# Gathering the experts' tokens in quarter rows with block transposes, and loading weights in 1 MB transfers

## The chip, the cores and the metric

The kernel runs on one core of a Trainium2 chip: TensorE (PE), VectorE (DVE), ScalarE (ACT), GpSimd (POOL), SyncE (SP) and 16 DMA engines. The metric is the device time of one execution in microseconds.

## The reference

One layer of a streaming encoder over 2048 tokens of width 1024: RMSNorm, one input projection, two groups of mixing heads (mLSTM and stick-breaking attention), an output projection, a mixture of experts, a gated per-layer term and a last RMSNorm. The part that matters here is the mixture of experts: every token goes to 2 of 32 experts, each expert is a SwiGLU of width 512.

```python
def expert_block(args):
    xb, e = args                                  # 128 rows of one expert
    hid = jax.nn.silu(xb @ w_gate[e]) * (xb @ w_up[e])
    return hid @ w_down[e]
y = lax.map(expert_block, (xin, block_e)).reshape(R, D)
out = jax.ops.segment_sum(y * buf_w[:, None], buf_tok, num_segments=T)
```

An expert has 6 MB of weights in float32: `w_gate` and `w_up` of 1024x512, `w_down` of 512x1024.

## The kernel before

All matmuls run in fp32r. A float32 operand is split into a high part (`hi`, a rounding copy on ScalarE, line 79) and a low part (`lo`, source minus `hi` on VectorE, line 80); a product is three matmuls, high by high, high by low, low by high (lines 88 to 90).

Phase 1 projects and runs the attention, phase 2 the mLSTM, the output projection and the router, phase 3 the experts, phase 4 the gated term and the output. Phase 2 writes the normed tokens to `c` in memory with four columns more: the two weights and the two experts of a token (line 834). At its end `route` builds tables of token indices: `toki` (whom to gather) and `tokd` (where to add), one column for each block of rows.

Phase 3 works on 47 blocks in a fixed order. The experts, ranked by their load, have fixed pieces: 128 rows, or 64 for the tail; 35 blocks have 128 rows and 12 have 64. Experts with several pieces and experts with one alternate. For each block:

- `xprep` (1079): GpSimd gathers the block's rows of `c` with one indirect DMA, one row of 4112 bytes to a partition, and forms the rows' weights `pw` with three tiny operations.
- `xturn` (1090): TensorE turns x in eight 128x128 transposes (1097) into two PSUM tiles, each of which is split into `xh` and `xl`.
- `gate_up` (1111): for each of 8 blocks of the width, 3 matmuls of 512 columns each for gate and up. In a block of 64 rows high and low lie side by side, 2 matmuls do, and the two halves of the result are added afterwards through `fold` tiles (1105).
- `hturn` (1139): the hidden rows are transposed by TensorE, four at a time, and split.
- `down` (1152): the product with `w_down`; the result goes to `y` and is added to `h` in memory by an indirect DMA of GpSimd (1174).

The loop over blocks (1205) interleaves them: in block b's `gate_up` the previous block's `hturn` stands before k = 3 and the next block's `xturn` before k = 6; after it comes the previous block's `down`. The scheduler of the framework may move instructions of an engine within the bounds of their inputs and buffers.

Weights come from `load_expert` (1071) on SyncE's queue: twelve pieces of 512 KB, each two blocks of 128 rows of gate or up (rows of 2 KB) or one of down (rows of 4 KB). `piece` (1250) lands one in one of five raw buffers (`wraw`: two in pool a, three in pool b), and splits it into `wh` and `wl`, 8 buffers each per pool. SyncE issues a load when VectorE has made `wl` of the piece that held the buffer.

After the experts `load4` (1262) loads the gate weights of phase 4 by the same `piece`, and a loop for overflowing experts follows that does not run on these inputs.

## Time and profile before

| | us |
|---|---|
| median of 3 runs | 2561.73 |
| lowest, highest | 2558.21, 2576.3 |
| profiled execution | 2559.68 |
| its span, first to last instruction | 2557.8 |

| engine | busy us of the span | share |
|---|---|---|
| TensorE matmuls | 2403.7 | 94% |
| VectorE | 1731.0 | 68% |
| ScalarE | 1294.0 | 51% |
| GpSimd | 657.5 | 26% |

The profile is of one execution, taken by the hardware profiler. A busy share is an average over stages with different limits; what an engine waited for is inferred from semaphores. Matmuls are pipelined, so a matmul's own duration is longer than the distance to the next. The expert stage runs from about 1540 to 2345 us of the span. A group's line gives the count, the busy time, the mean of one in ns, the engine's idle time just before them and what ended most of it. DMA packets are the rows that a transfer is cut into; a queue's share is the time that its packets took, over 16 engines.

### The profile page before, as it was taken

How to read it: one execution, taken by the hardware profiler on the slowest of the kernel's cores; microseconds unless marked ns; L12 is line 12 of the kernel's file. 1: busy time of each engine (PE TensorE's matmuls, PEld its weight loads, DVE VectorE, ACT ScalarE, POOL GpSimd, SP SyncE). 2: the span in 40 equal slices, each digit the busy share in tenths (PEclk: the TensorE clock that was granted, in tenths of full speed). 3: DMA queues.
4: the chain of work that ended last, by engine and by line, in shares of the span. 5: the costliest groups of instructions: out<-in, count | busy, mean ns of one | idle time of the engine just before them, and what ended most of it. 6: DMA issues, size and time to landing. Idle time of an engine off the chain costs nothing.

```text
span 2557.8 us, 36511 instructions
## 1 busy us (share of the span) xinstructions
PE 2403.7 (94%) x12620; PEld 1987.6 (78%) x12620; DVE 1731.0 (68%) x2628; ACT 1294.0 (51%) x2243; POOL 657.5 (26%) x777
## 2 busy tenths in 40 slices
PE   7899999999998899978999989999999999998998
PEld 6787787787876888967888767788877788786887
DVE  4488988988777445215555477777777787786665
ACT  5355656555555222223322366666666666675443
POOL 1122322322211230011111123232232333331654
PEclk9999999999999899989999999999999999998999
DMA  5776675675553532166666349999999999998332
GB/s 168 188 192 169 165 188 155 180 188 146 145 146 87 165 116 51 73 169 181 171 166 179 119 178 308 293 299 323 285 311 313 301 327 313 302 307 272 123 125 99
DMA packets 326038, 510.64 MB, mean 200 GB/s; under 512 B 40348, under 2 KB 163356, under 8 KB 324316
## 3 DMA queue, kind: packets, MB, share of 16 engines
q1 hardware_dynamic: 216044, 353.23, 42.2%
q0 software_dynamic: 97616, 123.05, 20.6%
q10 hardware_dynamic: 12192, 32.02, 3.5%
q8 instruction: 100, 1.64, 0.3%
q14 instruction: 86, 0.70, 0.1%
HBM read 389.63 MB, written 118.59 MB: 199 GB/s over the span
## 4 chain that ended last, share of the span: by engine, by line
PE 43%; DMA 11%; ACT 3%; issue 3%; DVE 3%; POOL 1%; SPq 0%; ACTq 0%; DVEq 0%; POOLq 0%
PE ppx L90 7%; PE ppx L88 7%; PE ppx L89 7%; DMA wraw<-in_w_exp_gate_dram 3%; DMA wraw<-in_w_exp_down_dram 3%; PE ps L88 2%; PE ps L90 2%; PE ps L89 2%; DMA md<-gr 2%; PE pw L89 2%; PE pw L90 2%; PE pw L88 2%; DMA wraw<-in_w_exp_up_dram 2%; ACT wh L79 2%; DVE wl L80 1%
## 5 line engine op out<-in xcount | busy, mean ns | idle before, releaser
L80 DVE TENSOR_TENSOR wl<-wraw,wh 128x1024 fp32r<-128x1024 f32 x384 | 458.9, 1219 | 132.6 <-ACT wh L79 129.1
L79 ACT CAST wh<-wraw 128x1024 fp32r<-128x1024 f32 x384 | 396.2, 1051 | 213.8 <-DMA wraw<-in_w_exp_gate_dram 78.7
L88 PE MATMUL ppx<-wh,xh 128*128 128x512 f32 x816 | 329.7, 405 | 5.8 <-ACT wh L79 5.0
L90 PE MATMUL ppx<-wh,xl 128*128 128x512 f32 x816 | 323.2, 396 | 2.8 <-DVE xl L80 2.7
L89 PE MATMUL ppx<-wl,xh 128*128 128x512 f32 x816 | 321.9, 395 | 0.5 <-DVE wl L80 0.5
L88 PE MATMUL ps<-aTh,whi 128*128 128x512 f32 x640 | 257.5, 403 | 6.6 <-ACT whi L79 3.3
L79 ACT CAST ph<-pt 128x512 fp32r<-128x512 f32 (+1 forms) x320 | 167.5, 523 | 180.1 <-PE pt L398 175.6
L90 PE MATMUL ps<-aTh,wlo 128*128 128x512 f32 x640 | 255.0, 398 | 0.7 <-DVE wlo L80 0.7
L89 PE MATMUL ps<-aTl,whi 128*128 128x512 f32 x640 | 255.5, 399 | 0.0
L385 DVE TENSOR_TENSOR_SCAN prod<-keep,prod,zeros 128x512 f32<-128x512 f32 x192 | 245.0, 1276 | 11.3 <-PE pt L398 5.8
L80 DVE TENSOR_TENSOR pl<-pt,ph 128x512 fp32r<-128x512 f32 (+1 forms) x320 | 190.1, 594 | 46.5 <-ACT ph L79 46.1
L380 ACT ACTIVATE keep<-pz 128x512 f32<-128x512 f32 (+2 forms) x320 | 171.5, 536 | 56.0 <-PE pz L378 46.7
L90 PEld LDWEIGHTS ppx<-wh,xl 128*128 128x128 f32 x816 | 154.1, 189 | 41.0 <-DVE xl L80 6.3
L88 PEld LDWEIGHTS ppx<-wh,xh 128*128 128x128 f32 x816 | 154.4, 189 | 40.0 <-ACT wh L79 5.3
L398 PE MATMUL pt<-ident,prod 128*128 128x128 f32 x1088 | 173.0, 274 | 11.6 <-DVE pl L80 10.1
L398 PEld LDWEIGHTS pt<-ident,prod 128*128 128x128 f32 x1088 | 134.0, 139 | 61.6 <-DVE pl L80 23.6
L89 PEld LDWEIGHTS ppx<-wl,xh 128*128 128x128 f32 x816 | 154.5, 189 | 33.3 <-DVE wl L80 1.0
L370 POOL DMA_DIRECT2D dv<-dv x80 | 60.9, 761 | 413.1 <-PE ot L411 338.6
L1174 POOL DMA_INDIRECT h<-y,tokd x47 | 119.8, 2550 | 164.1 <-DVE y L1173 63.4
L88 PE MATMUL ps<-whi,aTh 128*128 128x260 f32 (+1 forms) x512 | 145.0, 285 | 13.8 <-ACT whi L79 13.8
L88 PEld LDWEIGHTS ps<-aTh,whi 128*128 128x128 f32 x640 | 121.5, 190 | 32.6 <-ACT whi L79 4.3
L90 PEld LDWEIGHTS ps<-aTh,wlo 128*128 128x128 f32 x640 | 121.6, 190 | 31.2 <-DVE wlo L80 3.5
(320 smaller groups left out, 5439.6 us busy)
## 6 DMA issues: line engine op xcount, KB each, us to landing
wraw<-in_w_exp_gate_dram SPq DMA_DIRECT2D x128, 512.0 KB, 6.0
wraw<-in_w_exp_up_dram SPq DMA_DIRECT2D x128, 512.0 KB, 5.9
wraw<-in_w_exp_down_dram SPq DMA_DIRECT2D x128, 512.0 KB, 6.9
kt<-k POOLq DMA_DIRECT2D x80, 512.0 KB, 5.1
dv<-dv POOLq DMA_DIRECT2D x80, 256.0 KB, 3.4
k<-pst SPq DMA_DIRECT2D x64, 256.0 KB, 4.2
wraw<-in_w_in_dram SPq DMA_DIRECT2D x32, 256.0 KB, 4.1
q<-pst SPq DMA_DIRECT2D x32, 256.0 KB, 3.7
```

The source lines that it names most:

```text
L79: first = nc.scalar.copy(hi, src)
L80: nc.vector.tensor_sub(lo, src, f32(hi))
L88: mm(ps, lh, rh, start=start, stop=False)
L89: mm(ps, lh, rl, start=False, stop=False)
L90: return mm(ps, ll, rh, start=False, stop=stop)
L370: nc.gpsimd.dma_start(dv, self.dv2[m][4 * s:4 * s + 4, :, e, :].rearrange("i p d -> p i d"))
L380: nc.scalar.activation(kk[:, :w], ps[:, :w], AF.Sigmoid, scale=-0.125)
L385: nc.vector.tensor_tensor_scan(pr[:, :w][:, ::-1], kk[:, :w][:, ::-1], zeros[:, :w], 1.0 if s == t else carry[j][:, 0:1], ALU.mult, ALU.add)
L398: nc.tensor.transpose(pt[:, i * P:(i + 1) * P], pr[i][:, j * P:(j + 1) * P], self.ident)
L1174: nc.gpsimd.indirect_dma_start(out=self.hd_[:, :], out_offset=bass.IndirectOffsetOnAxis(ap=idx[:n], axis=0), in_=y[:n], in_offset=None, co ...
```

## The change

Five edits belong together.

1. Phase 2 writes the tokens to `c` with 1024 columns and the four extra columns to a tensor of their own, `inf`. `route` makes a table `qui` beside `toki`: for partition 32q + t and group g the index of quarter row q of token 32g + t of a block. Some tables move from a pool that lives on to one that ends with phase 2.
2. `xload` gathers a block's x by `qui`: for each 32 tokens one indirect DMA of 128 quarter rows of 1 KB, four in a block of 128 rows and two in one of 64, and one more for the 16 bytes of `inf`.
3. `xturn` is one VectorE transpose of 32x32 blocks into `xt` instead of eight on TensorE; ScalarE copies `xt` to `xh`, GpSimd subtracts to get `xl`. Partition p then holds columns 8p to 8p + 7 of x. `xt` and the `fold` tiles share one buffer. `turned` of block b + 1 stands before k = 2, and `load` of block b + 2 behind it.
4. So that rows of the weights match, gate and up are read with 8 neighbouring rows on a partition, down with 4; hidden columns are read with a stride of 4 from PSUM (`by4`). `pair` loads two pieces in one transfer of 1 MB, 8 KB in a row to a partition, into three raw buffers of 1 MB (one in pool a, two in b) instead of five of 512 KB, and splits each half as before.
5. `load4` loads the gate weights of phase 4 by `pair`.

```diff
-        self.cd_ = self.mk("c", [S, D + 4])
+        self.cd_ = self.mk("c", [S, D])
+        self.infd = self.mk("inf", [S, 4])
...
+        tab16 = t([P, NBLK], "r_tab", F16)
+        V.tensor_copy(tab16, tab[:, :NBLK])
+        tq = pp.tile([P, 4, NBLK], F32, name="pw")
+        for g in range(4):
+            nc.tensor.matmul(tq[:, g], sel[:, g].rearrange("p q t -> p (q t)"), tab16, start=True, stop=True)
+        quf = t([P, 4, NBLK], "r_quf")
+        V.tensor_scalar(quf, tq, 4.0, -4.0, op0=ALU.mult, op1=ALU.add)
+        qui = self.qui = c.tile([P, 4, NBLK], I32, name="qui")
+        V.tensor_scalar(qui, quf, 0.0, quart, op0=ALU.max, op1=ALU.add)
...
-                    src = a["w_exp_down"][0, bass.ds(ev, 1), q * P:(q + 1) * P, :]
-                    return self.piece(src.rearrange("e p n -> p (e n)"), [P, D], part)
-                src = a["w_exp_gate" if nm == "g" else "w_exp_up"][0, bass.ds(ev, 1), q * 256:(q + 1) * 256, :]
-                return self.piece(src.rearrange("e (c p) n -> p (e c) n", p=P), [P, 2, DE], part)
+                    src = a["w_exp_down"][0, bass.ds(ev, 1), :, :].rearrange("e (p k) n -> p (e k) n", p=P)
+                    return self.pair(src[:, 2 * q:2 * q + 2], [P, 2, D], [P, D], part)
+                src = a["w_exp_gate" if nm == "g" else "w_exp_up"][0, bass.ds(ev, 1), :, :]
+                src = src.rearrange("e (p k) n -> p (e k) n", p=P)
+                return self.pair(src[:, 4 * q:4 * q + 4], [P, 4, DE], [P, 2, DE], part)
...
-                xg = self.xgp.tile([P, D + 4], F32, name="xg")
-                nc.gpsimd.indirect_dma_start(out=xg[:n], out_offset=None, in_=self.cd_[:, :],
+                xg = self.xgp.tile([P, 4, D // 4], F32, name="xg")
+                for g in range(n // 32):
+                    nc.gpsimd.indirect_dma_start(out=xg[:, g], out_offset=None, in_=rows4,
+                                                 in_offset=bass.IndirectOffsetOnAxis(ap=qidx(g), axis=0))
+                inf = self.small.tile([P, 4], F32, name="xinf")
+                nc.gpsimd.indirect_dma_start(out=inf[:n], out_offset=None, in_=self.infd[:, :],
                                              in_offset=bass.IndirectOffsetOnAxis(ap=idx[:n], axis=0))
...
-                for q in range(2):
-                    ps = pp.tile([P, 4, P], F32, name="ppx")
-                    for j in range(4):
-                        k = 4 * q + j
-                        nc.tensor.transpose(ps[:, j, :n], xg[:n, k * P:(k + 1) * P], self.ident[:n, :n])
-                    ks = slice(4 * q, 4 * q + 4)
-                    if n == P:
-                        self.split(xh[:, ks], xl[:, ks], ps)
-                    else:
-                        self.split(xh[:, ks, :n], xh[:, ks, n:], ps[:, :, :n])
+                hi, lo = (xh, xl) if n == P else (xh[:, :, :n], xh[:, :, n:])
+                xt = wk.tile([P, KC, n], F32, name="xt", bufs=1)
+                nc.vector.transpose(xt.rearrange("p k (g t) -> p k g t", t=32),
+                                    xg[:, :n // 32].rearrange("p g (d k) -> p k g d", k=KC))
+                nc.scalar.copy(hi, xt)
+                nc.gpsimd.tensor_tensor(lo, xt, f32(hi), op=ALU.subtract)
...
-                        xg[b + 1] = prep(b + 1)
-
                         def turn_x(b=b):
-                            xT[b + 1] = xturn(xg[b + 1][0], work[b + 1][2])
-                        at[6] = turn_x
-                    hid[b] = gate_up(xT[b], xg[b][1], n, W[r], at)
+                            xT[b + 1] = turned(b + 1)
+                            if b + 2 < NB:
+                                xg[b + 2] = load(b + 2)
+                        at[2] = turn_x
+                    hid[b] = gate_up(*xT[b], n, W[r], at)
...
+    def pair(self, src, both, shape, part=None, scales=(None, None), halves=2):
+
+        n = self.npair = getattr(self, "npair", -1) + 1
+        raw = self.wps[part or "abb"[n % 3]].tile(both, F32, name="wraw", bufs=1 if (part or "abb"[n % 3]) == "a" else 2)
         self.nc.sync.dma_start(raw, src)
...
+            pool = self.wps[part or "ab"[v]]
+            hi = pool.tile(shape, F32R, name="wh")
+            lo = pool.tile(shape, F32R, name="wl")
+            self.split(hi, lo, u, scales[v])
+            out.append((hi, lo))
+        return out
```

## Rows read from the trace of the kernel before

**Rows 1.** stretches: us; busy PE, PEld, DVE, ACT, POOL; PEclk; DMA; GB/s
```profile
1540.00:1850.00 310.00, 306.96 (x1421) 248.49 (x1422) 228.63 (x244) 198.22 (x246) 87.30 (x93) 0.99 0.93 301
1850.00:2300.00 450.00, 438.73 (x2039) 349.92 (x2038) 349.32 (x379) 299.94 (x380) 139.00 (x131) 1.00 0.96 310
2300.00:2345.00 45.00, 43.40 (x195) 34.26 (x193) 32.30 (x35) 25.56 (x32) 5.58 (x3) 1.00 0.89 280
```

**Rows 2.** chain of waits, 1530 to 1860: start us, us, what
```profile
1675.79 0.87 PE ppx L1097 x8
...
1766.06 0.87 PE ppx L1097 x8
```

**Rows 3.** waits of SyncE, 1540 to 2300: us, times, longest
```profile
SPq L1255 <- DVE wl L80: 508.3, 357, 11.9
```

**Rows 4.** groups by line, 1530 to 2350: busy us, mean ns, idle before
```profile
L80 DVE TENSOR_TENSOR wl<-wraw,wh 128x1024 fp32r<-128x1024 f32 x384 | 458.9, 1219 | 132.6 <-ACT wh L79 129.1
...
L79 ACT CAST wh<-wraw 128x1024 fp32r<-128x1024 f32 x384 | 396.2, 1051 | 213.8 <-DMA wraw<-in_w_exp_gate_dram 78.7 <-DMA wraw<-in_w_exp_down_dram 63.5 <-DMA wraw<-in_w_exp_up_dram 49.5
...
L1174 POOL DMA_INDIRECT h<-y,tokd x47 | 119.8, 2550 | 164.1 <-DVE y L1173 63.4 <-issue 39.4 <-ACT wh L79 34.1
...
L1081 POOL DMA_INDIRECT xg<-c,toki x45 | 52.9, 1176 | 75.8 <-PE ppx L1097 69.2 <-issue 4.8 <-PE ppx L90 1.2
...
L80 DVE TENSOR_TENSOR xl<-ppx,xh 128x512 fp32r<-128x512 f32 x70 | 44.9, 684 | 10.7 <-ACT xh L79 10.7
...
L79 ACT CAST xh<-ppx 128x512 fp32r<-128x512 f32 x70 | 37.4, 586 | 5.7 <-PE ppx L1097 5.7
...
L1097 PE MATMUL ppx<-ident,xg 128*128 128x128 f32 x280 | 36.4, 272 | 2.7 <-DMA xg<-c,toki 2.7
...
L80 DVE TENSOR_TENSOR xh<-ppx,xh 128x256 fp32r<-128x256 f32 x24 | 8.9, 413 | 3.3 <-ACT xh L79 3.3
...
L1097 PE MATMUL ppx<-ident,xg 64*128 64x64 f32 x96 | 8.5, 229 | 0.0
```

**Rows 5.** timeline, last stage; then line 1344's min/median/max ns
```profile
2480.39 2.43 POOL L1331 TENSOR_TENSOR f_pl<-f_pl,gpost 128x1024 f32<-128x1024 f32 x1
...
2480.48 2.89 DVE L1344 TENSOR_TENSOR f_o<-f_o,f_h 128x512 f32<-128x512 f32 x1
...
L1344 DVE TENSOR_TENSOR f_o<-f_o,f_h x32: 676/693/2892, 2372.2 to 2550.8; 128x512 f32<-128x512 f32 x32
```

**Rows 6.** DMA at 1557:1567, 2354:2364, 1025.5:1031.5: packets, MB, share
```profile
q1 hardware_dynamic: 1749, 3.38, 101.1%
...
q1 hardware_dynamic: 984, 3.62, 100.1%
...
q1 hardware_dynamic: 144, 1.05, 43.2%
```

**Rows 7.** DMA queues, 1540 to 2345, the expert stage
```profile
q1 hardware_dynamic: 88120, 203.15, 72.1%
q0 software_dynamic: 11568, 41.50, 21.8%
```

**Rows 8.** DMA at 1681:1685.4, 995:1001, 1126:1136
```profile
q0 software_dynamic: 144, 0.53, 31.6%
...
q1 hardware_dynamic: 1056, 1.05, 64.2%
...
q0 software_dynamic: 2112, 1.05, 58.4%
```

**Rows 9.** timeline at the start of the expert stage
```profile
1532.49 0.42 SPq L1255 DMA_DIRECT2D wraw<-in_w_exp_gate_dram  x1
...
1534.32 1.29 DVE L80 TENSOR_TENSOR xl<-ppx,xh 128x512 fp32r<-128x512 f32 x2 [0.92 <-ACT xh L79]
...
1539.14 0.79 PE L88 MATMUL ppx<-wh,xh 128*128 128x512 f32 x1 [5.04 <-ACT wh L79]
```

**Rows 10.** DMA issues, whole span: count, median us to landing
```profile
xg<-c,toki POOLq DMA_INDIRECT x47, 8.1
```

More of the change, by code (lines that the diff above doesn't have):

```diff
@@ L860, in route @@
         nc.gpsimd.affine_select(tri, one, pattern=[[1, P]], base=0, channel_multiplier=-1, compare_op=ALU.is_gt, fill=0.0)
+        sel = t([P, 4, 4, 32], "r_sel", F16)
+        nc.gpsimd.tensor_copy(sel, self.ident.rearrange("p (g o t) -> p g o t", g=4, o=1).to_broadcast([P, 4, 4, 32]))
+        quart = t([P, 1], "r_quart")
+        for q in range(4):
+            nc.gpsimd.memset(quart[32 * q:32 * q + 32], float(q))
         seg = t([P, NE, NT], "r_seg")
@@ L1154, in down @@
                 y = wk.tile([P, D], F32, name="y")
+                t_ = folds() if n < P else None
                 for m in range(2):
@@ L1248, in phase3 @@
             self.phase4()
-    def piece(self, src, shape, part=None, scale=None):
-        n = self.npiece = getattr(self, "npiece", -1) + 1
-        u, v = (part, "a") if part else ("ab"[n % 2], "ababb"[n % 5])
-        raw = self.wps[v].tile(shape, F32, name="wraw", bufs=2 if v == "a" else 3)
+    def pair(self, src, both, shape, part=None, scales=(None, None), halves=2):
+        n = self.npair = getattr(self, "npair", -1) + 1
+        raw = self.wps[part or "abb"[n % 3]].tile(both, F32, name="wraw", bufs=1 if (part or "abb"[n % 3]) == "a" else 2)
         self.nc.sync.dma_start(raw, src)
-        hi = self.wps[u].tile(shape, F32R, name="wh")
-        lo = self.wps[u].tile(shape, F32R, name="wl")
-        self.split(hi, lo, raw, scale)
-        return hi, lo
+        out = []
+        w = both[1] // 2
+        for v in range(2):
+            u = raw[:, v * w:(v + 1) * w] if len(shape) == 3 else raw[:, v]
+            if v >= halves:
+                out.append(u)
+                continue
+            pool = self.wps[part or "ab"[v]]
[4 more added lines that the diff above has]
+        return out
     def load4(self):
@@ L1268, in load4 @@
         W = []
-        for k in range(N4):
-            with self.tc.issue_after(self.hsplit.ins) if k >= 1 else ExitStack():
-                W.append(self.piece(src[:, k], [P, D], "b", gl[:, k:k + 1]))
         rest = []
-        for k in range(N4, KC):
-            raw = wp.tile([P, D], F32, name="wraw", bufs=3)
-            nc.sync.dma_start(raw, src[:, k])
-            rest.append(raw)
+        for k in range(0, KC, 2):
+            with self.tc.issue_after(self.hsplit.ins) if k else ExitStack():
+                got = self.pair(src[:, k:k + 2], [P, 2, D], [P, D], "b", [gl[:, k + u:k + u + 1] for u in range(2)],
+                                min(2, max(0, N4 - k)))
+            for x_ in got:
+                (W if len(W) < N4 else rest).append(x_)
         pss = self.const2.tile([P, NT], F32, name="pss")
```

77 lines of the change are left out of this document (45 added, 32 removed).

## The prediction

> **What bounds the kernel now.** I read the stretches first, because the change only touches the expert stage. [rows 1] cut that stage into three stretches: together 805 us of the 2557.8 us span (1540 to 2345), with TensorE busy 789 of them and the 16 DMA engines at a share of 0.93, 0.96 and 0.89. The reader is to see two engines near their limit at once. VectorE is busy 610 of 805 us, ScalarE 524 and GpSimd 232. A busy TensorE is not by itself a bound, so I went to the chain of waits [rows 2]: from 1675.79 to 1766.06 it is made of matmuls alone and the eight transposes of x come back five times at a pitch of (1766.06 - 1675.79) / 5 = 18.05 us. In that part nothing but TensorE sets the time. From about 1850 on the chain also runs through weight loads, and there the DMA share is 0.96. So the stage is bound by TensorE in its first third and by TensorE and DMA almost equally afterwards. Who waits for whom on SyncE [rows 3] shows how the loads are held back: 508.3 us in 357 waits for VectorE's `wl`, which frees the raw buffer. The route, the attention and the last stage don't depend on the change, except at their edges.
>
> **The change part by part.**
>
> *x transposes leave TensorE.* A block loses the eight transposes of line 1097. In the chain they cost 0.87 us [rows 2]; 47 blocks (35 of 128 rows, 12 of 64; the counts 280 and 96 divided by 8 [rows 4]) give 47 x 0.87 = 41 us, all of it on the engine that sets the pace. TensorE's floor for the stage goes from 805 to 764 us; with the 16 us that it idles now (805 - 789) it is 780.
>
> *VectorE.* It loses the subtractions `xl`, 70 x 0.684 + 24 x 0.413 = 58 us [rows 4], and gets one 32x32-block transpose per block, which the trace does not show. The nearest row is `wl`, the same 128x1024 elements at 1.219 us [rows 4]; at worst the slowest 128x1024 operation in my rows, GpSimd's two-operand multiplication at 2.43 us [rows 5]. I take 1.22: 35 x 1.22 + 12 x 0.61 = 50 us, bounds 50 to 100. So -8 us, hidden behind VectorE's 195 idle us either way.
>
> *ScalarE.* Two copies of 0.586 us become one of 128x1024, as `wh` at 1.051 us [rows 4]: equal. The gate and up sums are now read with a stride; the trace has no price for that, so nothing, or at most a second pass of 0.586 us each; ScalarE's 281 idle us (805 - 524) hide it.
>
> *GpSimd.* Before, a block had one gather (1.176 us) and one scatter (2.550 us) [rows 4] beside three operations of two columns. Now it has five gathers (three in a block of 64 rows) and a two-operand subtraction, priced by the multiplication at 2.43 us [rows 5]: 5 x 1.18 + 2.55 + 2.43 = 10.9 us and the three, in a pitch of 18.05 - 0.87 = 17.2. It is no bound by its sum.
>
> *GpSimd against VectorE.* [rows 5] show what a two-operand GpSimd operation does to VectorE: the addition at 2480.48 took 2.89 us and ended 0.55 us after GpSimd's 2.43 us multiplication; the line's median is 0.693, its maximum 2.892. So a subtraction can hold VectorE's next `wl` for its whole length: at most 35 x 2.43 + 12 x 1.25 = 100 us in the stage, at least 0 when VectorE is elsewhere. VectorE is in `wl` 459 of 805 us [rows 4], 57%, so I take 60. It would then be busy 610 - 8 + 60 = 662 of 790 us, 84%: not the bound. Behind a held `wl` stand the release of the raw buffer and the next load [rows 3].
> The Trainium skill, "SBUF — State Buffer", section "SBUF: two separate sides", says the port pair that the two engines share is an exclusive lock, held for a whole instruction by whichever started first. The trace agrees, by the 2.89 us above. The rule speaks against this change; what it gives is the rival "VectorE becomes the bound" below.
>
> *Weights in longer rows.* Per expert 2048 rows of 2 KB and 512 of 4 KB become 768 of 8 KB. Prices per row from stretches where the loads saturate the engines [rows 6]: 2 KB: 101.1% x 10 us x 16 / (3.38 MB / 2048) = 98 ns; 4 KB: 100.1% x 160 / (3.62 MB / 4096) = 181 ns. Another 4 KB by the same slope gives 347 ns for 8 KB; bounds 324 (the lone 8 KB store, 43.2% x 6 x 16 / 128) and 362 (twice 181). The stage's queue [rows 7] spends 72.1% x 805 = 580 us on weights, 18.1 per expert; after: 768 x 347 / 16 = 16.7 us. That is -1.4 us, 32 x -1.4 = -45 us of DMA work. By the bounds 15.6 and 17.4 us per expert it is -80 to -23.
>
> *x in quarter rows.* A gather of 128 rows now costs 31.6% x 4.4 us = 1.39 us of all 16 engines [rows 8]. After it has 512 rows of 1 KB and 128 of 16 bytes. 1 KB: 64.2% x 6 x 16 / 1024 = 60 ns for a plain store; lower bound 324 / 8 = 41; upper bound twice the 512-byte rows of the software queue, 58.4% x 160 / 2048 = 46 ns, so 91 [rows 8]. I take 60, the same size, and 30 ns for the 16 bytes (0 to 60): 512 x 60 / 16 + 128 x 30 / 16 = 2.16 us. With 41 blocks' worth of rows (35 + 12 / 2): +32 us (-3 to +82).
>
> *DMA in all.* 72.1% + 21.8% of 805 is 756 us of work now; 756 - 45 + 32 = 743 after. At the share of 0.96 which the loaded stretch holds [rows 1] that needs 774 us.
>
> *Three raw buffers of 1 MB for five of 0.5 MB.* 3.0 MB may be under way instead of 2.5, but each is given back only when two splits are done: 1.05 + 1.05 + 1.22 = 3.3 us after landing instead of 2.3. At the stage's pace (6.3 MB per 18 us) 3.3 us are 1.15 MB held against 0.8: what is left in flight is equal. I cost it at 0; without that cover DMA's share would fall, which is in the range.
>
> *Start.* [rows 9]: the first weights are asked for at 1532.49 and TensorE starts at 1539.14, while x was ready at 1535.61 (1534.32 + 1.29). Now the first gate piece lands with its pair, and the first up piece behind 2 MB instead of 1: 1 MB more at 18.1 us per 6.3 MB is 2.9 us. x comes later too: three small steps on the route (about 1.5 us), four gathers where one was (3 x 1.18), the longer GpSimd step; some 7 us of which 3.5 were slack. Both are late by 3 to 4 us together, not one after the other: +4 (0 to 8).
>
> *The rest.* The table of quarter indices, with four small matmuls, is in the start above. The last stage's gate weights, now in pairs too, come in while the last blocks' matmuls run: 0, and 2.9 us, one MB, without that cover. The moves between pools issue nothing.
>
> **The sum.** TensorE wants 780 us, DMA 774. Blocks of an expert with two pieces lean on TensorE and those with one on DMA, so the stage is longer than either: I add half of TensorE's present idle, 8 us, to get 787 and 4 for the start: 791 against 805, -14. The profiled execution took 2559.68 us (2557.8 in the span, 1.9 around it), 2 below the median 2561.73. 2559.7 - 14 = 2546 us. Its own range is 2534 to 2560.
>
> **The rivals.**
> 1. *TensorE alone decides.* The 8 KB rows do better than the slope (324 ns) and the gathers cost no more: DMA work 756 - 80 = 676, far below TensorE. Then 764 plus half the idle plus 4 = 776: 2559.7 - 29 = 2531, at best 2523 with no idle. For it: the pure TensorE chain [rows 2]. Against: a share of 0.93 even there.
> 2. *The small rows eat the gain.* With 1 KB rows at 75 ns the gathers cost +52 and the weights give 23: 756 - 23 + 52 = 785 us of work, and 785 / 0.96 + 4 = 822 is 17 more than now: 2577. For it: from 2 to 4 KB a row's price per byte fell by 8% only. Against: 60 ns is a measured row of that size.
> 3. *VectorE becomes the bound* (slower). Place: the subtraction on GpSimd holds `wl`. Price: the full 100 us. VectorE then has 610 - 8 + 100 = 702 us of work; if the 129 us that it now waits for ScalarE before `wl` [rows 4], which is the weights' landing, all stay, the stage is 702 + 129 + 4 = 835: 2590. It decides once stalls and kept waits pass 805 - 602 = 203 us. Against: VectorE's two losses lie in waits that can overlap.
> 4. *x comes late each block* (slower). If GpSimd kept the text's order, subtraction of block b+1 ahead of the gathers of b+2, a loop closes: three gathers ahead 3.5, the fourth's landing 8.1 [rows 10], VectorE 1.22, ScalarE 1.05, GpSimd 2.43 and the scatter of 2.55 in the same queue: 18.9 us against a pitch of 17.2, 35 x 1.7 = 58 us in the blocks of 128 rows. From 780 + 4 that is 842: 2597, and more with any queueing. Against: the gathers now wait for the buffer that the transposes free (69.2 of 75.8 us of idle before them [rows 4]), so they go out about a block early.
>
> **How the numbers follow.** Forecast 0.42, rival 1 0.27, rival 2 0.11, rival 3 0.13, rival 4 0.07. 1% is 25.6 us, about what a measurement of this kernel can tell from no change: faster below 2534, slower above 2585. Faster: most of rival 1 (0.24) and the low end of the forecast (0.08), 0.32. Slower: rival 4 (0.07), rival 3 but for its lower end (0.11), and the upper end of rival 2 (0.04), 0.22. The rest, 0.46, is within 1%. The range takes in rival 1 to its best case and the prices of rivals 3 and 4: 2520 to 2598; outside is what queueing adds to those two, less than 0.2.
>
> **What would show it.** TensorE in the stage: no line 1097 and a pitch near 17.2 us in the first third; 17.2 everywhere would be rival 1. DMA: mean price of an 8 KB row near 347 ns, of a 1 KB gather row near 60 ns, share at 0.96 or more. VectorE: `wl` with a mean well above 1.219 us would be rival 3's stall, and its busy time in the stage 662 or 702. GpSimd: gathers issued right after the transposes, or after the subtraction (rival 4). I am wrong if the stage is shorter than 772 or longer than 800 us.

## The result, and the profile after

The changed kernel takes 2656.89 us in the median (2650.15 to 2662.45), the kernel before 2561.89 (2558.21 to 2576.3): a ratio of 1.0359, interval 1.0312 to 1.0405. It is slower by 95 us; the forecast was 2546 us, the range 2520 to 2598.

The profiled execution has a span of 2655.0 us, 97.2 more than before. From the first gather of x to the last scatter the stage takes 1528.5 to 2438.9, 910.4 us, against 818.0 (1527.5 to 2345.5). That is 92.4 of the 97.2; the last stage is 3.8 longer and the start of this one 1.0 later. From here on "the stage" is this distance.

The stretches of the expert stage after, in the columns of [rows 1]:

```profile
1540.00:1850.00 310.00, 264.61 (x1121) 212.38 (x1122) 226.85 (x204) 173.25 (x202) 217.41 (x170) 0.91 0.78 261
1850.00:2300.00 450.00, 395.65 (x1669) 314.13 (x1668) 348.89 (x316) 267.76 (x316) 298.46 (x222) 0.95 0.86 283
2300.00:2440.00 140.00, 121.59 (x498) 93.81 (x496) 106.66 (x100) 82.59 (x100) 63.91 (x41) 0.94 0.81 265
```

TensorE idles 118 of 900 us (900 - 782) where it idled 16 of 805 [rows 1]. Its granted clock falls from 0.99 and 1.00 to 0.91 to 0.95, lowest in the stretch in which it idles most (45 of 310 us); a granted 1 is the upper of its two levels, 2.4 GHz, and anything less is time at 1.2. So its busy time fell by only 7 us although 41 us of transposes are gone. No engine and no queue is as near its limit as TensorE was: TensorE 782 of 900 us, VectorE 682, DMA 0.78 to 0.86. A stage in which everybody has time is one in which they wait for each other. TensorE's longest waits, 1540 to 2440 (us in total, times, longest); in the stage of the kernel before no sum was over 5.0 us:

```profile
PE ppx L88 <- ACT wh L79: 32.0, 1, 32.0
PE ppx L90 <- DVE hl L80: 31.1, 15, 4.8
PE ppx L90 <- POOL xl L1129: 22.9, 7, 5.5
PE ppx L89 <- DVE wl L80: 17.6, 4, 6.6
```

The first is the start, the second the low part of the hidden values, the third the low part of x, the fourth that of the weights.

The DMA queues from 1540 to 2440, as [rows 7]:

```profile
q1 hardware_dynamic: 28419, 202.85, 62.7%
q0 software_dynamic: 14832, 41.71, 19.5%
```

That is 564 us of weights (580 before) and 176 us of gathers and scatters (175 before), 740 in all. DMA's work fell by 16 us: the longer weight rows gain, if less than forecast, and the queue with the small gathers costs as much as before.

The groups by line, 1538 to 2420, with the columns of [rows 4]:

```profile
L80 DVE TENSOR_TENSOR wl<-wraw,wh 128x1024 fp32r<-128x1024 f32 x383 | 486.3, 1307 | 106.4 <-ACT wh L79 106.2
...
L1105 POOL DMA_INDIRECT xg<-c,qui x157 | 224.1, 1428 | 101.0 <-DVE xt L1126 59.6 <-issue 34.0 <-PE ppx L90 6.1
...
L1129 POOL TENSOR_TENSOR xl<-xt,xh 128x1024 fp32r<-128x1024 f32 x35 | 86.1, 2460 | 7.9 <-ACT xh L1128 7.4
...
L1126 DVE STREAM_TRANSPOSE xt<-xg 128x1024 f32<-128x1024 f32 x35 | 76.5, 2185 | 85.9 <-POOL xh L1129 43.5 <-POOL xl L1129 33.8 <-DMA xg<-c,qui 8.6
```

Three things are to be read here. `wl` has a mean of 1.307 us instead of 1.219. VectorE's transpose takes 2.185 us, not 1.22. And VectorE stood 77 us (43.5 + 33.8) in front of its transposes of 128 rows, and 7 more in front of those of 64, until GpSimd had subtracted: the turned x has a single buffer (`xt`, bufs=1), which the subtraction gives back, and the subtraction waits in GpSimd's queue with the gathers.

Both kinds of wait can be seen singly. First the start, ScalarE's timeline with one line of VectorE's and one of GpSimd's:

```profile
1540.56 1.04 ACT L1128 CAST xh<-xt 128x1024 fp32r<-128x1024 f32 x1 [12.71 <-DVE xt L1126]
1556.63 1.04 ACT L1128 CAST xh<-xt 128x1024 fp32r<-128x1024 f32 x1 [15.02 <-DVE xt L1126]
1557.58 5.77 ACT L79 CAST wh<-wraw 128x1024 fp32r<-128x1024 f32 x6
...
1554.59 2.00 DVE L1126 STREAM_TRANSPOSE xt<-xg 128x1024 f32<-128x1024 f32 x1 [13.64 <-POOL xl L1129]
...
1552.21 2.35 POOL L1129 TENSOR_TENSOR xl<-xt,xh 128x1024 fp32r<-128x1024 f32 x1
```

The first x is cast at 1540.56. Its subtraction on GpSimd starts only at 1552.21, behind gathers of later blocks and an operation of 2.94 us for the last stage. So the second x is turned at 1554.59 and cast at 1556.63, and the first casts of weights stand behind that cast, at 1557.58, although all three raw buffers had been asked for by 1530.93. TensorE runs without a break from 1563.77, 35 us after the first gather at 1528.50; before it was 1539.14 [rows 9], 11.7 us after the gather at 1527.47.

Second the stall, VectorE's, ScalarE's and GpSimd's timelines between 1657 and 1670:

```profile
1664.98 4.10 DVE L80 TENSOR_TENSOR wl<-wraw,wh 128x1024 fp32r<-128x1024 f32 x1
...
1657.64 1.05 ACT L1128 CAST xh<-xt 128x1024 fp32r<-128x1024 f32 x1
...
1657.94 1.54 POOL L1105 DMA_INDIRECT xg<-c,qui  x1 [0.30 <-issue]
1659.78 1.49 POOL L1105 DMA_INDIRECT xg<-c,qui  x1 [0.30 <-issue]
1661.58 1.96 POOL L1105 DMA_INDIRECT xg<-c,qui  x1 [0.30 <-issue]
1663.84 1.43 POOL L1105 DMA_INDIRECT xg<-c,qui  x1 [0.30 <-issue]
...
1665.57 2.42 POOL L1129 TENSOR_TENSOR xl<-xt,xh 128x1024 fp32r<-128x1024 f32 x1
1667.93 1.20 POOL L1116 TENSOR_TENSOR pw<-pw,xinf 128x2 f32<-128x2 f32 x1
```

One `wl` takes 4.10 us while GpSimd subtracts, and ends 1.09 us after the subtraction, about as long as a `wl` alone takes. [rows 5] show the same, only that there VectorE's operation began after GpSimd's and here 0.59 us before it. The lines show the wait too: the cast that the subtraction reads had ended at 1658.69, and four gathers stood ahead of the subtraction. Over the 47 blocks it starts 3.6 us in the median after its cast has ended, 10.6 at most.

### The profile page after: what moved, and what is told of

It is laid out like the page before. It is cut to its first block, busy times and chain, and to the rows that moved or that the text cites. A ratio compares the mean times of both kernels' runs of the same rounds, so it can differ in the third digit from the quotient of the medians.

```text
span 2655.0 us, 35019 instructions
## 1 busy us (share of the span) xinstructions
PE 2393.7 (90%) x12248; PEld 1972.8 (74%) x12248; DVE 1797.3 (68%) x2584; ACT 1287.8 (49%) x2196; POOL 1011.9 (38%) x993
## 4 chain that ended last, share of the span: by engine, by line
PE 32%; DMA 12%; DVE 7%; issue 6%; POOL 5%; ACT 3%; DVEq 0%; POOLq 0%; SPq 0%; ACTq 0%
DMA wraw<-in_w_exp_down_dram 5%; DVE wl L80 4%; PE ppx L90 4%; PE ppx L89 4%; PE ppx L88 4%; PE ps L88 2%; POOL xg L1105 2%; DMA wraw<-in_w_exp_gate_dram 2%; PE ps L90 2%; PE ps L89 2%; PE pw L89 2%; PE pw L90 2%; PE pw L88 2%; DMA md<-gr 2%; ACT wh L79 1%
## 5 line engine op out<-in xcount | busy, mean ns | idle before, releaser
L80 DVE TENSOR_TENSOR wl<-wraw,wh 128x1024 fp32r<-128x1024 f32 x384 | 487.4, 1306 | 106.4 <-ACT wh L79 106.2
L79 ACT CAST wh<-wraw 128x1024 fp32r<-128x1024 f32 x384 | 386.9, 1048 | 230.0 <-DMA wraw<-in_w_exp_up_dram 90.8
L1105 POOL DMA_INDIRECT xg<-c,qui x164 | 230.8, 1407 | 103.1 <-DVE xt L1126 59.6
L72 POOL TENSOR_TENSOR rs_r<-rs_v,neghalf 128x1 f32<-128x1 f32 (+1 forms) x80 | 55.6, 694 | 320.1 <-DVE rs_v L70 320.1
L1126 DVE STREAM_TRANSPOSE xt<-xg 128x1024 f32<-128x1024 f32 (+1 forms) x47 | 90.7, 1930 | 93.1 <-POOL xh L1129 43.5
```

Of the source, the lines that this page charges most:

```text
L72: nc.gpsimd.tensor_tensor(r, v, self.neghalf[:, :width], op=ALU.pow)
L79: first = nc.scalar.copy(hi, src)
L80: nc.vector.tensor_sub(lo, src, f32(hi))
L1105: nc.gpsimd.indirect_dma_start(out=xg[:, g], out_offset=None, in_=rows4, in_offset=bass.IndirectOffsetOnAxis(ap=qidx(g), axis=0))
L1126: nc.vector.transpose(xt.rearrange("p k (g t) -> p k g t", t=32), xg[:, :n // 32].rearrange("p g (d k) -> p k g d", k=KC))
```

## The experiments

Three theories were put up. A: the wait, through the turned buffer and GpSimd's queue. B: three raw buffers of 1 MB hold less in flight than five of 0.5. C: GpSimd's subtraction stalls VectorE's `wl`. A fourth question was why nothing was gained. Times are medians; ratios are against the kernel before, with their 95% interval.

### The subtraction on VectorE

```diff
-                nc.gpsimd.tensor_tensor(lo, xt, f32(hi), op=ALU.subtract)
+                nc.vector.tensor_tensor(lo, xt, f32(hi), op=ALU.subtract)
```

> The changed kernel with one engine swapped: the subtraction that makes x's low part runs on VectorE instead of GpSimd. Theory A (the single buffer of turned x is given back by GpSimd's subtraction, which stands in GpSimd's queue behind the gathers; VectorE waited 84 us for it at its transposes, the start alone came 24.6 us later): the wait disappears and most of the 95 us come back, 2565 to 2590 us. Theory B (three raw buffers of 1 MB hold less in flight than five of 0.5 MB; SyncE waited 725.6 us for wl instead of 508.3): the loads are as they were, at most 25 us come back, 2630 or more. Theory C (GpSimd's subtraction stalls VectorE's wl, mean 1.307 instead of 1.219 us): wl falls to 1.22 us, that is 34 us of VectorE, against 35 x 1.2 + 12 x 0.6 = 49 us that it takes over: 2650 to 2670.

2586.76 us, 1.0099 (1.0079 to 1.0119): this one line is 70 of the 95 us. `wl` in the groups by line:

```profile
L80 DVE TENSOR_TENSOR wl<-wraw,wh 128x1024 fp32r<-128x1024 f32 x384 | 454.8, 1217 | 106.4 <-ACT wh L79 106.0
```

TensorE's two longest sums of waits, 1540 to 2440 (us in total, times, longest):

```profile
PE ppx L90 <- DVE hl L80: 41.0, 12, 5.9
PE ppx L88 <- ACT wh L79: 21.7, 1, 21.7
```

B falls as the main cause: the buffers are the same. A and C both lose their object here; the fall of `wl` to 1.217 is C's, the vanished wait is A's. What is left is the wait for the split of the hidden values, which rose from 31.1 to 41.0 us now that VectorE has the subtraction too (2.8 in the kernel before), and 22 us at the start.

### A subtraction on GpSimd that nobody waits for

To part A from C, a kernel with the subtraction on VectorE (the one of "the turn later", below) got a second, idle one.

```diff
+                if n == P:
+                    nc.gpsimd.tensor_tensor(wk.tile([P, KC, P], F16, name="dummy", bufs=1), f32(xl), f32(hi), op=ALU.subtract)
```

> The kernel with the subtraction on VectorE and the late turn (2579.28 us, wl 1.218 us in the mean, none above 1.4) with a second subtraction of the same size on GpSimd, into a scratch tile that nobody reads, 35 times. No engine waits for its result, so it has the price of GpSimd's place and of its stall of VectorE alone. If these are what the subtraction on GpSimd cost (theory C): wl's mean rises to 1.29 or more with single calls of 3 to 4 us, and the time by 30 us or more, 2610 to 2650. If the dependence is what cost (x's low part and the turned buffer waiting behind gathers, theory A): 2577 to 2592.

2618.88 us, 1.0219 (1.0201 to 1.0236): 40 us more than its base, as theory C expected. The groups by line:

```profile
L80 DVE TENSOR_TENSOR wl<-wraw,wh 128x1024 fp32r<-128x1024 f32 x384 | 517.3, 1383 | 63.3 <-ACT wh L79 55.2 <-issue 5.8 <-PE ppx L1157 1.6
...
L1131 POOL TENSOR_TENSOR dummy<-xl,xh 128x1024 f16<-128x1024 f32 x35 | 88.6, 2531 | 9.9 <-DVE xl L1129 9.2
```

VectorE loses 384 x (1.383 - 1.218) = 63 us to 89 us of GpSimd's work, and 40 us arrive in the time. Nothing depends on the idle result, VectorE's wait for gathers at its transposes is what it was (16.4 us, 16.3 in the base), and it waits for no result of GpSimd's, so C is real. The Trainium skill, "SBUF — State Buffer", section "SBUF: two separate sides", gives the rule for it, an exclusive lock that is held for the whole instruction by whichever engine started first. The trace agrees that the one waits for the whole of the other: all 20 `wl` over 1.5 us in the changed kernel, and all 30 here, end 1.08 to 1.10 us after a subtraction. Who goes first can't be read from the start times: the `wl` of 4.10 us above was held although it began before the subtraction.

How much of the 70 us is C's this run does not show. In the changed kernel `wl` loses 384 x 0.088 = 34 us, little more than half of the 63; at this run's rate, 40 / 63, that would be some 21 us, an estimate. The rest of the 70 would then be A's, with what it costs at the start.

### The start's order

In the changed kernel the second x's cast and VectorE's share of its turning were put behind the fourth of the first expert's weight splits; nothing else was touched.

```diff
...
-                            xT[b + 1] = turned(b + 1)
+                            with ExitStack() as first:
+                                if b == 0:
+                                    first.enter_context(tc.issue_after(early[0].ins))
+                                    first.enter_context(tc.issue_after(early[1].ins))
+                                xT[b + 1] = turned(b + 1)
```

> The changed kernel with only the order at the stage's start altered: ScalarE's cast of the second x (and VectorE's part of its turning) is put behind the first casts of weights. In the changed kernel that cast stood ahead of them and waited 15.0 us for the single turned buffer, so the first weights, landed by 1539, were cast from 1557.6 on. If this order is the start's loss, the first cast comes near 1541 and 12 to 18 us come back: 2638 to 2646 us, with the rest of the stage as it was. If the start is late for another reason (the gathers themselves): 2652 to 2660.

2648.02 us, 1.0348 (1.0323 to 1.0373): 9 us back, under the 12 to 18 expected, and the runs overlap (2642.44 to 2657.55, against 2650.15 to 2662.45), so the 9 is rough. ScalarE's timeline shows that the order did what it should:

```profile
1542.14 1.04 ACT L1128 CAST xh<-xt 128x1024 fp32r<-128x1024 f32 x1 [12.72 <-issue]
1543.09 5.77 ACT L79 CAST wh<-wraw 128x1024 fp32r<-128x1024 f32 x6
```

The weights are cast 14.5 us earlier, but the first expert then waits for its low part of x, which GpSimd still makes late (the first matmul with `xl` runs at 1558.2). There TensorE waits 12.0 us for it. So the order is some 9 us of the loss, and GpSimd's queue holds most of the rest of the start.

### The x part alone, and with a second turned buffer

The x path of the change with the weights in five buffers of 512 KB again, gate and up now in rows of 4 KB; then the same with `xt` (and the folds that share its space) in two buffers.

```diff
-                    return self.pair(src[:, 2 * q:2 * q + 2], [P, 2, D], [P, D], part)
+                    return self.piece(src[:, q], [P, D], part)
...
-                return self.pair(src[:, 4 * q:4 * q + 4], [P, 4, DE], [P, 2, DE], part)
+                return self.piece(src[:, 2 * q:2 * q + 2], [P, 2, DE], part)
...
```
```diff
-                xt = wk.tile([P, KC, n], F32, name="xt", bufs=1)
+                xt = wk.tile([P, KC, n], F32, name="xt", bufs=2)
```

> The changed kernel's x path (quarter gathers, VectorE's transposes, GpSimd's subtraction) with the weights again in transfers of 512 KB into five buffers, now with rows of 4 KB on each partition. Theory A: the wait for GpSimd is untouched, 2640 to 2665 us. Theory B: five buffers are back, the stage returns to its old length, 2560 to 2580. Theory C: 2640 to 2665, with wl again near 1.31 us.

> The kernel of the x part alone (2688.65 us) with one more buffer of 4 KB a partition for turned x, so that VectorE's next transpose need not wait for GpSimd's subtraction; GpSimd keeps the subtraction. There VectorE waited 76 us for GpSimd at the transposes and ScalarE's casts stood behind them. If the single buffer is the coupling (theory A): those waits go, the first expert matmul starts some 15 us earlier, 2600 to 2630 us. If it is the place of the subtraction in GpSimd's queue or its stall of wl (theory C), TensorE waits on for xl (47 us there) and wl keeps single calls of up to 4 us: 2670 to 2690 us.

2688.65 us, 1.0507 (1.0486 to 1.0528), and 2665.26, 1.0392 (1.0357 to 1.0427). The first was expected at 2640 to 2665 by A and C and at 2560 to 2580 by B, and is slower than all of them. Five buffers didn't help; but the rows of 4 KB cost more too (below), so it is the weights part alone, below, that refutes B. The second buffer gave 23 us, less than A had expected and more than C had. VectorE's waits for GpSimd at the transposes fell from 76 us to 45:

```profile
DVE xt L1124 <- POOL xl L1127: 39.1, 10, 6.4
...
DVE xt L1124 <- POOL xh L1127: 6.3, 1, 6.3
```

They stayed that long because the subtraction still comes late in GpSimd's queue, 5.7 us in the median after its cast has ended, and TensorE still waited 43 us for x's low part. So 23 us is what a second buffer gives, and not all that A costs; how the 70 us divide between A and C stays open.

### The weights part alone

The kernel before with 1 MB transfers, 8 KB rows and three raw buffers. In the first form c is stored with its columns reordered to match, in the second TensorE's transposes read every eighth column. The weights' edits are those of the change; the edits for x:

```diff
-                nc.vector.scalar_tensor_tensor(ct, xt, r, gf, op0=ALU.mult, op1=ALU.mult)
+                nc.vector.scalar_tensor_tensor(ct.rearrange("p (k q) -> p q k", k=KC), xt.rearrange("p (q k) -> p q k", k=KC), r,
+                                               gf.rearrange("p (q k) -> p q k", k=KC), op0=ALU.mult, op1=ALU.mult)
```
```diff
-                        nc.tensor.transpose(ps[:, j, :n], xg[:n, k * P:(k + 1) * P], self.ident[:n, :n])
+                        nc.tensor.transpose(ps[:, j, :n], xg[:n, :D].rearrange("p (q k) -> p k q", k=KC)[:, k], self.ident[:n, :n])
```

> The kernel before with the weights part alone: 1 MB transfers, rows of 8 KB, three raw buffers; x is gathered whole, one gather a block, and turned by TensorE as before (c is stored with its columns reordered so that the partitions match). Theory A: no loss comes from here; an 8 KB row costs 364 ns in the changed kernel, 17.5 us an expert instead of 18.1, so 20 us less DMA work: 2540 to 2565. Theory B: the loss is here: 2610 to 2650, and SyncE's waits for wl stay near 700 us. Theory C: as A.

> The weights part alone again, without reordering c: TensorE's transposes read every eighth column of x instead. In the first form c's VectorE operation rose from 1.284 to 2.035 us and the stage began 15 us later (first gather at 1542.9 instead of 1527.5), while the stage itself was as long as before (816.4 against 818.0 us). If the strided read costs TensorE nothing: 2555 to 2564 us, no change to the kernel before. If it costs twice a transpose, 41 us more of TensorE: 2590 to 2605.

2575.91 us, 1.0071 (1.0042 to 1.01), and 2565.89, 1.0011 (0.9997 to 1.0025). In the first form all of the loss is ahead of the stage (the reordered store below, 2.035 us where the changed kernel has 1.284); the stage itself takes 816.4 us. The first lay 11 us above what A and C expected and far below B's 2610, the second 2 us above its 2555 to 2564. In the second the stage takes 818.0 us, as before.

```profile
L702 DVE SCALAR_TENSOR_TENSOR ct<-wst,rs_r,gf 128x1024 f32<-128x1024 f32 x5 | 10.2, 2035 | 3.4 <-POOL rs_r L72 3.4
```

The stretches of the second form:

```profile
1540.00:1850.00 310.00, 309.53 (x1423) 251.94 (x1424) 229.94 (x244) 197.66 (x246) 90.05 (x92) 0.99 0.90 301
1850.00:2300.00 450.00, 444.53 (x2043) 358.29 (x2042) 351.90 (x381) 299.88 (x380) 146.19 (x131) 0.99 0.93 310
2300.00:2345.00 45.00, 41.97 (x189) 33.24 (x187) 34.34 (x35) 29.11 (x35) 6.72 (x3) 1.00 0.87 272
```

DMA's share falls from 0.96 to 0.93 in the middle stretch, TensorE stays busy 796 of 805 us, and the time doesn't move; in the first form, with TensorE's transposes as before, the stage doesn't move either. So a share of 0.96 was no bound, the stage before was TensorE's, and three buffers of 1 MB were enough: B is refuted.

### Rows of 4 KB, two ways

The kernel before with 512 KB transfers and five buffers, the gate and up rows 4 KB long: once 16 KB from start to start, in the arrangement of the change, once end to end.

```diff
-                src = a["w_exp_gate" if nm == "g" else "w_exp_up"][0, bass.ds(ev, 1), q * 256:(q + 1) * 256, :]
-                return self.piece(src.rearrange("e (c p) n -> p (e c) n", p=P), [P, 2, DE], part)
+                src = a["w_exp_gate" if nm == "g" else "w_exp_up"][0, bass.ds(ev, 1), :, :]
+                src = src.rearrange("e (p k) n -> p (e k) n", p=P)
+                return self.piece(src[:, 2 * q:2 * q + 2], [P, 2, DE], part)
```
```diff
-                return self.piece(src.rearrange("e (c p) n -> p (e c) n", p=P), [P, 2, DE], part)
+                return self.piece(src.rearrange("e (p k) n -> p (e k) n", p=P), [P, 2, DE], part)
```

(The first reorders c, as the first form above; the second reads x's columns with a stride.)

> The kernel before with one thing changed: the weights' rows. Five buffers and 512 KB transfers as before, but the gate and up weights come with 4 KB on a partition in one row instead of two of 2 KB. By the prices of the kernel before (98 ns for 2 KB, 181 for 4 KB) 2048 rows of 2 KB become 1024 of 4 KB, 2048 x 98 / 16 - 1024 x 181 / 16 = 1.0 us an expert, 31 us of DMA work in the stage. If DMA bounds the later two thirds of the stage: 2540 to 2552. If TensorE alone does: 2558 to 2564. No theory sees a loss here.

> The kernel before with rows of 4 KB for gate and up in another arrangement: a transfer of 512 KB covers 256 adjacent rows of the matrix, two on a partition, so its rows of 4 KB lie end to end, while in the run before with 4 KB they lay 16 KB apart (stage 836.0 against 818.0 us, 2.93 us of all DMA engines per MB against 2.86). If the spacing was the loss: under 2.8 us per MB, 2545 to 2562 us. If rows of 4 KB are the loss: 2.93 us per MB, 2572 to 2585.

2594.53 us, 1.0147 (1.0117 to 1.0177), a stage of 836.0; and 2566.08, 1.0008 (0.9994 to 1.0021), a stage of 821.1. The weights' queue from 1560 to 2340 with the spaced rows:

```profile
q1 hardware_dynamic: 53009, 193.03, 72.4%
```

and end to end:

```profile
q1 hardware_dynamic: 53966, 196.53, 71.3%
```

72.4% x 780 / 193.03 is 2.93 us of all engines per MB, 71.3% x 780 / 196.53 is 2.83; 2.86 before [rows 7]. Rows of 4 KB gain 1% of DMA work end to end and nothing in time, between the two expectations. 16 KB apart they are a loss, 18 us in the stage; the rest of the 33 us lies ahead of it, where c is reordered. No theory had expected that. The x part alone reads the same spaced rows (65.1% x 880 / 195.08 = 2.94 us per MB from 1560 to 2440) and the whole change 8 KB rows from the same places at 564 / 202.85 = 2.78, which is a likely reason why the x part alone was the slower one; no run shows that apart. Nor do these runs show why spacing costs.

### What keeps the rest: the turn later, and the start again

On the kernel with the subtraction on VectorE the next x is turned at the seventh step of a block instead of the third, so that VectorE splits the hidden values first; then the start's order of above on top of that.

```diff
-                        at[2] = turn_x
+                        at[6] = turn_x
```

> The changed kernel with the subtraction on VectorE (2586.76 us) and one thing more: the turning of the next x stands at the seventh step of a block instead of the third, so that the split of the hidden values (hl) comes ahead of transpose and subtraction in VectorE's queue. TensorE waited 41.0 us for hl there, against 3.9 us with the weights part alone. If that order is what is left of the loss: hl's wait falls below 15 us and the time to 2555 to 2572 us. If VectorE is simply too full (82 to 88 us busy in 100): the wait moves to xl or wl and the time stays at 2580 to 2592.

> The kernel with the subtraction on VectorE and the late turn (2579.28 us, first cast of weights 17.4 us after the first gather, against 10.5 in the kernel before) with the start's order altered as in the run on the changed kernel. If that order is what is left of the start's loss: the first cast comes about 12 us after the first gather and the time is 2571 to 2576 us. If VectorE's transposes and gathers set it: 2577 to 2583.

2579.28 us, 1.0073 (1.0048 to 1.0099); then 2571.99, 1.0047 (1.003 to 1.0065). The wait for the hidden values fell from 41.0 us to this:

```profile
PE ppx L90 <- DVE hl L80: 11.8, 11, 1.6
```

Each found some 7 us, close to what these runs can tell apart: the first fell short of the 2555 to 2572 expected, the second came as expected. The stage is now 822.9 us, and still it is no shorter than before. The stage before and the stage of this last kernel, from first gather to last scatter:

```profile
1527.47:2345.53 818.06, 793.83 (x3673) 635.88 (x3671) 618.15 (x667) 530.12 (x668) 239.17 (x235) 0.99 0.94 305
...
1529.12:2352.02 822.90, 757.89 (x3284) 601.43 (x3284) 700.43 (x667) 523.79 (x615) 518.57 (x396) 0.98 0.91 303
```

TensorE has 36 us less to do and idles 41 us more, 65 instead of 24.

### Why the 41 us don't arrive

Three runs on that last kernel (2571.99 us): half of the weights' bytes with all engine work kept; six buffers of 512 KB for three of 1 MB; the second copy of the output on ScalarE.

```diff
...
-        self.nc.sync.dma_start(raw, src)
+        self.nc.sync.dma_start(raw if full else raw[:, :w], src if full else src[:, :w])
...
+            z = v if full else 0
-            u = raw[:, v * w:(v + 1) * w] if len(shape) == 3 else raw[:, v]
+            u = raw[:, z * w:(z + 1) * w] if len(shape) == 3 else raw[:, z]
```
```diff
+                src = src.rearrange("e (f c d k) n -> c f (e d) (k n)", f=4, c=4, k=2)
...
-        raw = self.wps[part or "abb"[n % 3]].tile(both, F32, name="wraw", bufs=1 if (part or "abb"[n % 3]) == "a" else 2)
+        raw = self.wps[v].tile(shape, F32, name="wraw", bufs=3)
...
+        if quarters:
+            for f in range(4):
+                self.nc.sync.dma_start(raw[32 * f:32 * f + 32], src[f])
```
```diff
-                        if m:
-                            nc.vector.tensor_copy(y[:, ms], py)
-                        else:
-                            nc.scalar.copy(y[:, ms], py)
+                        nc.scalar.copy(y[:, ms], py)
```

> The kernel with the subtraction on VectorE, the late turn and the start's order (2571.99 us). It leaves out half of every weight load: of each 1 MB transfer only the first half comes, and both halves of its hi and lo parts are made from it, so all work of the engines stays and the weights' bytes halve. If the loads (their bytes and the three buffers) take the gain: the stage falls towards TensorE's floor, 2571.99 - 30 or more, 2520 to 2542 us. If VectorE and ScalarE in order do: 2562 to 2572 us.

> The same kernel with six raw buffers of 512 KB for three of 1 MB. The gate and up weights come as four transfers of 128 KB for each buffer (32 partitions by 4 KB, rows end to end), since one transfer with four outermost strides ran at 137 GB/s. If the coarse buffers hold the loads back: the DMA share rises from 0.92 to 0.95 and the time falls to 2548 to 2566 us. If not, or if the additional transfers cost what they gain: 2570 to 2590.

> The same kernel with the second copy of each 128-row block's output moved from VectorE (35 x 0.683 = 24 us) to ScalarE, which is busy 64 us in 100. If VectorE's fullness takes the gain: 2555 to 2567 us. If the loads do: 2569 to 2575.

Half the bytes: 2549.91 us, 0.9954 (0.9937 to 0.997), a stage of 796.5, between the two expectations. Two of its stretches, and the stage:

```profile
1540.00:1850.00 310.00, 304.00 (x1332) 247.16 (x1332) 272.76 (x255) 204.42 (x238) 221.88 (x173) 0.98 0.67 185
1850.00:2300.00 450.00, 429.67 (x1878) 342.85 (x1877) 404.97 (x388) 301.43 (x361) 343.89 (x209) 0.99 0.68 184
...
1528.10:2324.59 796.49, 751.75 (x3284) 603.56 (x3284) 698.90 (x667) 520.60 (x615) 583.50 (x396) 0.98 0.68 186
```

With DMA at 0.68, TensorE still idles 20 of 450 us in the second stretch and 45 in the stage, and VectorE is busy 405 of 450. So half of the loads' bytes stand for 22 us of time and for 20 of the 41 us that TensorE idles more; the other half of the 41 stays. That it is lost between engines that run their queues in order is argued, not shown. Taking 24 us off VectorE gave nothing (2573.38 us, 1.0054, 1.0026 to 1.0082, as expected if the loads take the gain); with the loads as they are VectorE's fullness alone is not it. Which of the two would have to go first, or how much both together would give, these runs don't settle.

The finer buffers tell nothing on that: 2891.74 us, 1.1266 (1.1238 to 1.1294), because in transfers of 32 partitions the loads themselves are dearer, 68.7% x 900 / 160.21 = 3.86 us per MB from 1600 to 2500:

```profile
q1 hardware_dynamic: 53662, 160.21, 68.7%
```

A first form, on the kernel with the turn later, had one transfer for each buffer of gate or up weights, with the four quarters as its outermost stride:

```diff
+                return self.piece(src[q], [P, 2, DE], part, quarters=True)
...
         self.nc.sync.dma_start(raw, src)
```

> The kernel with the subtraction on VectorE and the late turn (2579.28 us) with six raw buffers of 512 KB for three of 1 MB, the same space, in rows of 4 KB; the weight rows are dealt to the partitions so that 32 neighbouring partitions read 128 KB end to end, and x's transpose is made in two halves to match. There SyncE waited 675 us for wl at a DMA share of 0.91 and a TensorE share of 0.95. If the coarse buffers hold the loads back: the DMA share rises to 0.94 or more and the time falls to 2550 to 2568. If the rows of 4 KB cost what they did 16 KB apart (2.93 us per MB against 2.77): 2580 to 2595.

3546.81 us, 1.3845 (1.3813 to 1.3877). The weights' queue from 1600 to 3200:

```profile
q1 hardware_dynamic: 47057, 181.38, 34.7%
```

All DMA together runs at 137 GB/s there, and the queue's packets fill 34.7% of the engines' time while ScalarE waits 1007 of the 1600 us for gate and up weights. The Trainium skill, "DMA: Bandwidth & Descriptors", section "Rules for kernel authors", says that an outermost dimension of fewer than 16 confines a transfer to at most so many of the engines. Four of 16 would fit this run; no row here shows the engines one by one.

No version that does the whole work beats the kernel before.

## Why the prediction was wrong, point by point

The step that failed is the move of the subtraction to GpSimd. It stands in the sum at nothing: its stall of VectorE was taken as covered by VectorE's idle time, and the wait for its result was not priced at all. Put back on VectorE it gave 70 of the 95 us.

**What bounds the kernel.** "Bound by TensorE in its first third and by TensorE and DMA almost equally afterwards" was wrong in its second half. The weights part alone took 18 us of DMA work away (69.8% of 805 us instead of 72.1%) and the stage stayed at 818.0 us. I took a share of 0.96 for a limit because loads appeared in the chain; TensorE's 16 idle us in 805 [rows 1] were the row to go by.

**x transposes leave TensorE.** The work went: no line 1097, 41 us. But the busy time fell from 789 to 782 us, since the time that it idles came with a lower granted clock. The step's price was about right (36 us less in the last kernel above, at nearly the old clock) and its effect was not, because the sum takes the stage as TensorE's work plus a small allowance for idle time. That holds only if everything TensorE waits for comes as early as it did, and the change had just lengthened the way from gather to x. The sum also counts the 16 idle us twice: 805 - 41 = 764 holds them already, so 780 is 16 too many by the step's own reckoning. Mended, the forecast would have lain further off still.

**VectorE.** The transpose was taken at 1.22 us, the nearest row; it measured 2.185 (1.186 in 64-row blocks), 91 us in all against 50, within the bounds of 50 to 100. "Hidden behind VectorE's 195 idle us" is a cover that fell: the idle time lies in front of `wl` and the transposes, where VectorE waits for others, and with the subtraction off GpSimd an order on VectorE alone (the turn later) was worth some 7 us.

**ScalarE.** The strided read of the gate sums cost nothing from PSUM (0.593 us, 0.604 before), as taken; in the blocks of 64 rows, where it reads the folded sums in SBUF, it went from 0.629 to 1.138 us, 12 times, 6 us in all.

**GpSimd against VectorE.** The mechanism was named and bounded; 60 us were assumed and 34 measured (384 x 0.088). What failed is again the cover. I set 662 of 790 us against full and concluded that it was not the bound; 63 us of stall cost 40 us of time in the run with the idle subtraction. Behind a stalled `wl` stand a raw buffer and all that follows in VectorE's queue, and idle time elsewhere doesn't make up for that. The rival "VectorE becomes the bound" had the place right and the condition wrong: it was to decide only once stalls and kept waits passed 203 us. They came to 34 + 106 = 140, and TensorE waited all the same.

**The wait through the turned buffer.** No step priced it. The diff shows a single `xt`, freed by an operation of GpSimd, and the prediction costed that subtraction only as work. It is the missing term: 77 us of VectorE's waits and 23 us of TensorE's for `xl`. A second buffer alone gave 23 us, on the x part alone; what the whole wait costs is not measured apart. The fourth rival came nearest, since it chained gathers, transpose, cast and subtraction into a loop, but it made the gathers late; they went out early, and the subtraction stood behind them, as between 1657 and 1666 above.

**Start.** +4 (0 to 8) was forecast, by landings. The gathers and weights landed about as said; TensorE started its run 24 us later: a cast of the second x stood first in ScalarE's queue, and that x waited for the subtraction in GpSimd's. The step asked when data comes and not what stands ahead of it in the queue. ScalarE's order alone was worth some 9 us, and 7 with the subtraction on VectorE.

**Weights in longer rows, quarter rows.** 8 KB rows measured 62.7% x 900 x 16 / (202.85 MB / 8192) = 365 ns, above 347 and just past the upper bound of 362: -16 us, not -45. The quarter rows cost 0, not +32. That the sum of DMA work came out right, 740 us against 743 forecast, is luck: two errors that cancel. Neither made the kernel slower.

**The buffers.** "Equal, at 0" can't be told apart from the rest in the changed kernel; with the weights part alone it was right, SyncE waited longer in the same stretch (619 us instead of 508 [rows 3]) and nothing was late.

**The sum of it.** Of the 95 us the subtraction on GpSimd is 70, and how these divide is open: the stall of 63 us that cost 40, the start's order with 9 and the second buffer with 23 were measured on three different kernels, and their sum of 72 proves nothing. The other 25 are order on VectorE (7), the start (7), and 10 us over the kernel before that are left when both are mended. Slower by over 1% had a chance of 0.22, and the dearest rival stood at 2597. Each rival had one cause at work; here several worked together.

## What to carry to other kernels

With TensorE busy 98% the stage was TensorE's, at a DMA share of 0.96 too; taking work off such an engine gains only if all that it waits for stays as early as it was. Work moved to an idle engine is costed by three things, what stands ahead of it in that engine's queue, which buffer it gives back and who stands behind that buffer, and what it locks while it runs; here GpSimd, idle most of the time before, was a place for the 47 subtractions that cost 70 us more than the busy VectorE. Before covering a cost with an engine's idle time, look at what ends that idle time: here the time that VectorE spent waiting for the chain covered nothing.

## What was unexpected of the hardware

- VectorE's 32x32-block transpose of 128x1024 float32, reading with a stride of eight, took 2.185 us where a two-operand subtraction of the same size took 1.217. Writing with a stride (c reordered) raised another VectorE operation from 1.284 to 2.035 us.
- A read with a stride of four cost nothing from PSUM (ScalarE 0.593 us, before 0.604; VectorE 0.735, before 0.742) and a good half more from SBUF (ScalarE 1.138 us, before 0.629; VectorE 1.134, before 0.744).
- TensorE's transposes that read every eighth column hardly cost more: 0.278 us in the mean instead of 0.272 in blocks of 128 rows, 0.277 instead of 0.229 in those of 64, and the stage was 818.0 us either way.
- 1 KB gathers from c seem to cost no more for a byte than whole 4 KB rows: the software queue had 176 us in the stage, 175 before, with the same scatters in it.
- Weight rows of 4 KB that start 16 KB apart cost 2.93 us of all DMA engines per MB, end to end 2.83, and 8 KB rows 2.78.
- A transfer of 512 KB dealt as four outermost strides took the stage's rate to 137 GB/s, and four transfers of 32 partitions each cost 3.86 us per MB.
